# Two residual blocks with MLA and RWKV7 mixers: the FFN's first products by Strassen's scheme on pairs of tiles

## Chip, cores and metric

One Trainium2 chip, one of its cores (core 0). The metric is the device time of one execution in microseconds (us); lower is better. TensorE is the matmul engine, VectorE, ScalarE and GpSimd work on tiles, SyncE issues most transfers.

## Reference

Two blocks on x of 512 tokens by 1024 features, all in float32. Each block is an FFN, a mixer and a second FFN, each behind an RMS norm with a shift and a scale and with a gate that come from a vector c through `ada_w` (the modulation). The first block's mixer is latent attention (MLA), the second's RWKV7. An FFN is what the change is about:

```python
def _swiglu(h, w_in, w_out):
    gt, up = jnp.split(h @ w_in, 2, axis=-1)
    return (jax.nn.silu(gt) * up) @ w_out

x = x + 0.5 * mods[:, 0, 2][:, None, :] * _swiglu(h, w_in, w_out)
```

`h` has 1024 features, the inner width is 2816, so `w_in` is 1024 x 5632 and `w_out` 2816 x 1024. The program has four FFNs, one after the other with the mixers between: FFN, MLA, FFN, FFN, RWKV7, FFN.

## The kernel before, in words

Activations lie feature-major: a tile has 128 features on the partitions and 512 tokens along it. 1024 features are 8 tiles (`KT`), the inner width is 22 (`NF`). Float32 accuracy comes from splitting every operand into a high part and a rest (`float32r`) and adding three products: high by high, high by rest, rest by high (`mm3`, L268 to L274). So each product of a weight tile and an activation tile is three matmuls, and each matmul has its own weight load. A run of up to eight weight tiles of 128x128 (1024 columns) is loaded into a slot of `wraw` (three slots) by SyncE's queue (L245 to L249), ScalarE writes its high part `wh` (L262) and VectorE the rest `wl` (L266); `wh` and `wl` have three slots each.

An FFN (`ffn`, L477) goes in two halves of 11 inner tiles. For two inner tiles at a time it runs gate and up (u = 0, 1): 8 weight tiles of each, all 512 tokens, into four banks of PSUM (L502 to L504). ScalarE takes the silu of the gate (L507), VectorE multiplies it by up (L508), and `split` (L276) writes the high part (ScalarE, L279) and the rest (VectorE, L280) as `act`. After a half, `down` (L394) forms the eight output tiles from the 11 `act` tiles and adds each, times its gate, to x (`add_x`, L390 to L392). So x gets two additions for each of its tiles in an FFN. In the second half the last two output tiles go by halves of the tokens (256 columns, weights kept by `tail_weights`), so that the next norm's first half can start while the second half of them is multiplied; the last matmuls cover the norm (`_Norm.half`). The first products of the next FFN are by halves of the tokens too (L497 to L500). In the first FFN, the first four inner tiles come from `start` (L1481), which lays out norm, loads and products by hand.

The modulation vectors are 128 further tiles of 128x1024 (`mod_steps`, L359): each is loaded into a slot of `wraw` and reduced by one VectorE instruction with an accumulator (L366). `pump` (L381) issues them in small numbers between the pairs and the output tiles of the FFNs, until none is left.

Outside `start`, the last tiles before RWKV and RWKV itself, the order in which each engine takes its instructions is laid out by a scheduler when the program is built, from the order of the program and from the slots that are free; on the chip each engine keeps that order. Slots are shared by tag: `t` has 22 slots of two tiles (x, h, act and others), `s` 18 of one tile, `k` two of three tiles, and the PSUM tags `A` to `D` two banks each (L38). The numbers of a pair's products and the banks they go to:

```python
order = [(k, f, u, slice(0, S)) for f in fs for u in range(2) for k in range(KT)]
for k, f, u, sl in order if w else ():
    self.mm3(p[f, u], w[f, u][0][:, k], w[f, u][1][:, k], h[k], k == 0, k == KT - 1, sl)
```

## Time and profile before

| | |
|---|---|
| time, median of three runs | 2253.03 us (2250.35 to 2255.33) |
| span of the profiled execution, first to last instruction | 2255.1 us |
| TensorE busy | 96% |
| VectorE, ScalarE, GpSimd busy | 56%, 37%, 14% |
| mean granted clock of TensorE | 0.983 of 2.4 GHz |

The profile records the span of its execution, which lies inside the range of the runs; no other time is given for that execution. PE in the rows is TensorE's matmuls, PEld its weight loads, DVE VectorE, ACT ScalarE, POOL GpSimd, SP SyncE. A busy time counts an instruction from its start to its end, and instructions that are pipelined overlap: the start of one to the start of the next tells what it costs in a row. A matmul is busy for 0.39 us at 512 columns and 0.28 at 256, which is its latency. "x2" in a timeline merges two instructions of a kind. PEclk is the granted clock as a share of 2.4 GHz.

### The profile page before, as it was taken

The numbers are of one execution on the slowest core, as the hardware profiler recorded it, in microseconds if no ns is written. First come the engines' busy times: TensorE is split into PE (matmuls) and PEld (weight loads), VectorE is DVE, ScalarE is ACT, GpSimd is POOL, SyncE is SP. The second block draws the span as 40 slices with busy tenths as digits, with TensorE's granted clock in tenths as the row PEclk, the third lists the DMA queues.
The fourth block names the chain that finished last, engine by engine and source line by source line (L and its number), as shares of the span: only waits on it lengthen the run. The fifth ranks groups of instructions, "written<-read, shape, count | busy, mean of one in ns | idle before, by whom it ended". The sixth has DMA issues, their size and how long they took to land.

```text
span 2255.1 us, 29276 instructions
## 1 busy us (share of the span) xinstructions
PE 2165.5 (96%) x11089; PEld 1825.0 (81%) x11089; DVE 1252.3 (56%) x2247; ACT 841.7 (37%) x1403; POOL 324.9 (14%) x370
## 2 busy tenths in 40 slices
PE   6999999999999999999999998899789999999998
PEld 5778888878798888888888887677678879888887
DVE  8655555678665545556433337936946666333334
ACT  3322223467533222333222225756445444222222
POOL 5000001023200000010000003514575000000001
PEclk9999999999999999999999999999889999999999
DMA  8665666201325656645433332254686342323322
GB/s 283 196 196 171 203 202 192 81 32 34 129 85 191 200 180 203 189 131 168 126 99 103 95 108 88 75 168 142 181 245 165 96 146 85 95 86 110 96 84 82
DMA packets 150732, 312.25 MB, mean 138 GB/s; under 512 B 54784, under 2 KB 70432, under 8 KB 150592
## 3 DMA queue, kind: packets, MB, share of 16 engines
q1 hardware_dynamic: 149856, 309.68, 44.7%
q8 instruction: 87, 1.43, 0.3%
q10 hardware_dynamic: 576, 0.52, 0.1%
q14 instruction: 53, 0.43, 0.1%
q0 software_dynamic: 160, 0.19, 0.0%
HBM read 279.93 MB, written 30.41 MB: 138 GB/s over the span
## 4 chain that ended last, share of the span: by engine, by line
PE 82%; DVE 9%; DMA 3%; ACT 3%; issue 2%; POOL 1%; SPq 0%; DVEq 0%; ACTq 0%; POOLq 0%
PE up L272 13%; PE up L274 13%; PE up L273 13%; PE dn L272 8%; PE dn L273 8%; PE dn L274 8%; PE pr L168 4%; PE q L168 2%; PE a L168 2%; PE s L168 1%; PE o L168 1%; DVE ada L168 1%; DVE rsq_u L168 1%; PE ys L168 1%; DMA wraw<-in_ffn_in_dram 1%
## 5 line engine op out<-in xcount | busy, mean ns | idle before, releaser
L262 ACT ACTIVATE wh<-wraw 128x1024 fp32r<-128x1024 f32 (+2 forms) x307 | 292.8, 954 | 919.6 <-PE dn L273 274.4
L272 PE MATMUL up<-h,wh 128*128 128x512 f32 (+1 forms) x1416 | 536.3, 379 | 1.9 <-ACT silu L507 1.9
L273 PE MATMUL up<-h,wh 128*128 128x512 f32 (+1 forms) x1416 | 536.5, 379 | 0.0
L274 PE MATMUL up<-h,wl 128*128 128x512 f32 (+1 forms) x1416 | 535.9, 379 | 0.0
L266 DVE TENSOR_TENSOR wl<-wraw,wh 128x1024 fp32r<-128x1024 f32 (+2 forms) x307 | 334.6, 1090 | 325.4 <-ACT wh L262 322.5
L272 PEld LDWEIGHTS up<-h,wh 128*128 128x128 f32 x1416 | 266.7, 188 | 51.9 <-ACT silu L507 2.3
L273 PEld LDWEIGHTS up<-h,wh 128*128 128x128 f32 x1416 | 266.8, 188 | 49.7
L274 PEld LDWEIGHTS up<-h,wl 128*128 128x128 f32 x1416 | 266.4, 188 | 49.7
L366 DVE SCALAR_TENSOR_TENSOR wraw<-wraw,cact 128x1024 f32<-128x1024 f32 x128 | 158.0, 1235 | 180.5 <-DMA wraw<-in_ada_w_dram 179.4
L65 POOL TENSOR_TENSOR sq<-sq,sq 128x512 f32<-128x512 f32 x29 | 39.8, 1373 | 1494.3 <-ACT sq L61 1478.9
L272 PE MATMUL dn<-act,wh 128*128 128x512 f32 x627 | 244.7, 390 | 2.7 <-ACT act L279 2.7
L273 PE MATMUL dn<-act,wh 128*128 128x512 f32 x627 | 244.6, 390 | 0.3 <-DVE act L280 0.3
L274 PE MATMUL dn<-act,wl 128*128 128x512 f32 x627 | 244.7, 390 | 0.0
L272 PEld LDWEIGHTS dn<-act,wh 128*128 128x128 f32 x627 | 118.1, 188 | 27.8 <-ACT act L279 3.1
L273 PEld LDWEIGHTS dn<-act,wh 128*128 128x128 f32 x627 | 118.1, 188 | 25.2 <-DVE act L280 0.6
L274 PEld LDWEIGHTS dn<-act,wl 128*128 128x128 f32 x627 | 118.0, 188 | 24.5
L508 DVE TENSOR_TENSOR silu<-silu,up 128x512 f32<-128x512 f32 x88 | 60.2, 685 | 127.6 <-PE up L274 126.2
L392 DVE SCALAR_TENSOR_TENSOR x<-dn,mod,x 128x512 f32<-128x512 f32 (+1 forms) x91 | 61.6, 678 | 119.4 <-PE dn L274 119.1
L168 DVE TENSOR_TENSOR wl<-wraw,wh 128x1024 fp32r<-128x1024 f32 (+2 forms) x51 | 57.3, 1126 | 64.9 <-ACT wh L168 64.6
L168 PE MATMUL pr<-xs,wh 128*128 128x512 f32 (+1 forms) x242 | 78.0, 404 | 8.9 <-ACT xs L168 3.6
L279 ACT ACTIVATE act<-silu 128x512 fp32r<-128x512 f32 x88 | 55.2, 628 | 50.3 <-DVE silu L508 49.3
L168 PEld LDWEIGHTS pr<-xs,wh 128*128 128x128 f32 x242 | 47.0, 205 | 18.4 <-ACT xs L168 3.7
(414 smaller groups left out, 3494.9 us busy)
## 6 DMA issues: line engine op xcount, KB each, us to landing
wraw<-in_ffn_in_dram SPq DMA_DIRECT2D x168, 512.0 KB, 3.8
wraw<-in_ada_w_dram SPq DMA_DIRECT2D x128, 512.0 KB, 3.8
wraw<-in_ffn_out_dram SPq DMA_DIRECT2D x64, 384.0 KB, 3.1
wraw<-in_ffn_out_dram SPq DMA_DIRECT2D x64, 320.0 KB, 2.9
wraw<-in_rwkv_rkv_dram SPq DMA_DIRECT2D x24, 512.0 KB, 3.6
ada<-in_ada_w_dram SPq DMA_DIRECT2D x16, 512.0 KB, 6.0
bakd<-bak SPq DMA_DIRECT2D x32, 192.0 KB, 3.9
bak<-bakd SPq DMA_DIRECT2D x8, 768.0 KB, 6.3
```

What stands on the lines that cost most here:

```text
L65: nc.gpsimd.tensor_tensor(self.acc, self.acc, sq, op=ALU.add)
L168: self.tc.keep_in_program_order(op(*args, **kw))
L262: self.nc.scalar.activation(wh[:, :n], raw[:, :n], AF.Copy)
L266: self.nc.vector.tensor_tensor(wl[:, :n], raw[:, :n], wh[:, :n], op=ALU.subtract)
L272: mm(ps, wh, ah, start=first, stop=False)
L273: mm(ps, wh, al, start=False, stop=False)
L274: mm(ps, wl, ah, start=False, stop=last)
L279: nc.scalar.activation(hi[rows, sl], src, AF.Copy)
L366: nc.vector.scalar_tensor_tensor(raw2, raw2, 1.0, self.cact, op0=ALU.mult, op1=ALU.mult, accum_out=m[:, j - j0:j - j0 + 1])
L392: self.nc.vector.scalar_tensor_tensor(x, ps[:, sl], g[:, m:m + 1], x, op0=ALU.mult, op1=ALU.add)
L508: nc.vector.tensor_tensor(sl, sl, p[f, 1], op=ALU.mult)
```

## The change

Pairs of inner tiles are multiplied by Strassen's scheme (in Winograd's form). For gate and for up, the weights of a pair are a 2 x 2 matrix of quarters (two inner tiles by two halves of the 1024 features), and h is one of two halves of the features by two halves of the tokens. Seven products of quarters take the place of eight: each is 4 weight tiles by 256 tokens. The sums of weight quarters (s1 to s4) are formed by GpSimd and then split into high part and rest; the sums of activation quarters are formed once in an FFN by `activation_sums` (GpSimd rebuilds h from its parts, VectorE subtracts and splits). Products are accumulated in three banks X, Y and Z; between them ScalarE copies a bank to SBUF (c11, c12, p5, c22) and VectorE or GpSimd adds.

Pair 0 of each FFN stays as it was (`pair_plain`), and so do the pairs 0 and 1 of the first FFN, which come from `start`. The second product is done in five parts of two, two, two, two and three pairs (`PARTS`); the first four use `down_part`, which loads the weights of two output tiles at once, the last uses `down` as before with 6 inner tiles for 11. The raw weights of the second tile of a pair take a slot of the tag `k`. `wh` and `wl` get five slots for three; to make room, two small tiles of MLA move to the tag `s` and GpSimd's scratch for transfers shrinks, with the five setup loads moving from GpSimd's queue to ScalarE's. Cut to its core (comments that were removed are left out):

```diff
+PARTS = (0, 1), (2, 3), (4, 5), (6, 7), (8, 9, 10)
...
-        wh = self.wp.tile([P, 8, P], F32R, name=f"wh_{self.n}", tag="wh", bufs=3)
-        wl = self.wp.tile([P, 8, P], F32R, name=f"wl_{self.n}", tag="wl", bufs=3)
+        wh = self.wp.tile([P, 8, P], F32R, name=f"wh_{self.n}", tag="wh", bufs=5)
+        wl = self.wp.tile([P, 8, P], F32R, name=f"wl_{self.n}", tag="wl", bufs=5)
...
     def ffn(self, l, j, norm, nxt):
-        nc = self.nc
         s = 2 * j
-        h = norm.h
-        for half in range(2):
+        done = NS // 2 if norm.first else 1
+        for part in PARTS:
             act = []
-            f_end = (half + 1) * NH
-            f0 = half * NH
-            while f0 < f_end:
-                fs = range(f0, min(f0 + 2, f_end))
-                w, p = {}, {}
-                if f0 == 0 and norm.first:
-                    fs, p = range(NS), norm.first
+            for g in part:
+                if g == 0:
+                    self.pair_plain(l, j, norm, act)
+                elif g < done:
+                    self.pair_out(norm.first, 2 * g, act)
                 else:
-                    for f in fs:
-                        for u in range(2):
-                            first = f0 == 0 and norm.w
-                            w[f, u] = norm.w.pop(0) if first else self.wchunk(self.a["ffn_in"][l, j, f, u], KT)
-                            p[f, u] = self.ps("up", ("AB", "CD")[(f0 - half * NH) // 2 % 2][u])
-                if f0 == 0:
-                    order = [(k, f, u, HALF[0]) for k in range(KT) for f, u in THREE]
-                    order += [(k, f, u, HALF[1]) for k in range(KS) for f, u in THREE]
-                    order += [(k, f, u, HALF[1]) for f, u in THREE for k in range(KS, KT)]
-                    order += [(k, 1, 1, slice(0, S)) for k in range(KT)]
-                else:
-                    order = [(k, f, u, slice(0, S)) for f in fs for u in range(2) for k in range(KT)]
-                for k, f, u, sl in order if w else ():
-                    self.mm3(p[f, u], w[f, u][0][:, k], w[f, u][1][:, k], h[k], k == 0, k == KT - 1, sl)
-                for f in fs:
-                    sl = self.t("silu")
-                    nc.scalar.activation(sl, p[f, 0], AF.Silu)
-                    nc.vector.tensor_tensor(sl, sl, p[f, 1], op=ALU.mult)
-                    act.append(self.split(sl, "act", "u" if len(act) < 4 else "t"))
-                f0 += len(fs)
-                self.pump(4 if f0 > 2 else 0)
-
-            def chunks(m, half=half):
+                    self.pair_seven(l, j, g, norm, act)
+                self.pump(4 if g else 0)
+            k0, n = 2 * part[0] * P, 2 * len(part)
+            def chunks(m, k0=k0, n=n):
                 w = self.a["ffn_out"][l, j, m]
-                k0 = half * NH * P
-                return [(w[:, k0:k0 + 6 * P], 6), (w[:, k0 + 6 * P:k0 + NH * P], NH - 6)]
-
-            if half == 0:
-                self.down(chunks, act, (l, s))
+                if part is PARTS[-1] and (l, j) == (1, 0):
+                    return [(w[:, k0 + i * P:k0 + (i + n // 2) * P], n // 2) for i in (0, n // 2)]
+                return [(w[:, k0:k0 + n * P], n)]
+            if part is not PARTS[-1]:
+                self.down_part(self.a["ffn_out"][l, j], part[0] * 2, act, (l, s))
             else:
                 tail = (7,) if (l, j) == (1, 0) else (6, 7)
                 nx = nxt(tail)
                 self.down(chunks, act, (l, s), nx, tail)
         return nx
 
+    def down_part(self, w, f0, act, key):
+        self.mods_until(self.gate, key)
+        g, n = self.gate[key], len(act)
+        for m in range(0, KT, 2):
+            self.n += 1
+            raw = self.wp.tile([P, 8, P], F32, name=f"wraw_{self.n}", tag="wraw", bufs=3)
+            self.nc.sync.dma_start(raw.rearrange("p (m k) f -> p m (k f)", m=2),
+                                   w[m:m + 2, :, f0 * P:(f0 + n) * P].rearrange("m p f -> p m f"))
+            wh, wl = self.wsplit(raw, 2 * n)
+            for i in range(2):
+                ps = self.ps("dn", "ABC"[(m + i) % 3])
+                for k in range(n):
+                    self.mm3(ps, wh[:, i * n + k], wl[:, i * n + k], act[k], k == 0, k == n - 1)
+                self.add_x(m + i, ps, g)
+            self.pump(1)
+    def pair_out(self, p, f0, act):
+        nc = self.nc
+        for f in (f0, f0 + 1):
+            sl = self.t("silu")
+            nc.scalar.activation(sl, p[f, 0], AF.Silu)
+            nc.vector.tensor_tensor(sl, sl, p[f, 1], op=ALU.mult)
+            act.append(self.split(sl, "act", "u" if len(act) < 4 else "t"))
+    def pair_plain(self, l, j, norm, act):
+        h, p = norm.h, norm.first
+        if not p:
+            w, p = {}, {}
+            for f in range(2):
+                for u in range(2):
+                    w[f, u] = norm.w.pop(0) if norm.w else self.wchunk(self.a["ffn_in"][l, j, f, u], KT)
+                    p[f, u] = self.ps("up", ("AB", "CD")[f][u])
+            self.activation_sums(norm)
+            order = [(k, f, u, HALF[0]) for k in range(KT) for f, u in THREE]
+            order += [(k, f, u, HALF[1]) for k in range(KS) for f, u in THREE]
+            order += [(k, f, u, HALF[1]) for f, u in THREE for k in range(KS, KT)]
+            order += [(k, 1, 1, slice(0, S)) for k in range(KT)]
+            for k, f, u, sl in order:
+                self.mm3(p[f, u], w[f, u][0][:, k], w[f, u][1][:, k], h[k], k == 0, k == KT - 1, sl)
+        else:
+            self.activation_sums(norm)
+        self.pair_out(p, 0, act)
+    def activation_sums(self, norm):
+        nc, h = self.nc, norm.h
+        norm.sums7 = []
+        for i in range(KT // 2):
+            b = []
+            for k in (i, i + KT // 2):
+                b.append(self.t("hs"))
+                nc.gpsimd.tensor_tensor(b[-1], h[k][0].bitcast(F32), h[k][1].bitcast(F32), op=ALU.add)
+            norm.sums7.append(self.quarter_sums([x[:, sl] for x in b for sl in HALF]))
+    def quarter_sums(self, b):
+        nc = self.nc
+        b11, b12, b21, b22 = b
+        t = [self.t("ts").rearrange("p (a s) -> p a s", a=2) for _ in range(2)]
+        t1, t2, t3, t4 = (t[i // 2][:, i % 2] for i in range(4))
+        for out, x, y in ((t1, b12, b11), (t2, b22, t1), (t3, b22, b12), (t4, b21, t2)):
+            nc.vector.tensor_tensor(out, x, y, op=ALU.subtract)
+        hi, lo = (self.t2(n, F32R, "t").rearrange("p a (b s) -> p (a b) s", b=2) for n in ("tsh", "tsl"))
+        for i in range(2):
+            r = slice(2 * i, 2 * i + 2)
+            nc.scalar.activation(hi[:, r], t[i], AF.Copy)
+            nc.vector.tensor_tensor(lo[:, r], t[i], hi[:, r], op=ALU.subtract)
+        return [(hi[:, i], lo[:, i]) for i in range(4)]
+    def pair_seven(self, l, j, g, norm, act):
+        nc, free = self.nc, self.nc
+        K2 = KT // 2
+        q0, q1 = slice(0, K2), slice(K2, KT)
+        W = []
+        for u in range(2):
+            src = [self.a["ffn_in"][l, j, 2 * g + i, u].rearrange("p (k f) -> p k f", f=P) for i in range(2)]
+            ra = self.wraw(src[0], KT)
+            self.n += 1
+            rb = self.gp.tile([P, KT, P], F32, name=f"wrawb_{self.n}", tag="k", bufs=TAGS["k"])
+            nc.sync.dma_start(rb, src[1])
+            W.append((ra, rb))
+        w = [{} for _ in range(2)]
+        def keep(u, hl, *names):
+            for i, name in enumerate(names):
+                w[u][name] = tuple(x[:, i * K2:(i + 1) * K2] for x in hl)
+        sub = lambda out, x, y: nc.gpsimd.tensor_tensor(out, x, y, op=ALU.subtract)
+        S = []
+        for u, (ra, rb) in enumerate(W):
+            keep(u, self.wsplit(ra, KT), "a11", "a12")
+            st = self.t2("ws", F32, "t").rearrange("p a (k f) -> p (a k) f", f=P)
+            s2, s1 = st[:, q0], st[:, q1]
+            nc.gpsimd.tensor_tensor(s1, rb[:, q0], rb[:, q1], op=ALU.add)
+            sub(s2, s1, ra[:, q0])
+            sub(rb[:, q0], ra[:, q0], rb[:, q0])
+            S.append((st, s2))
+        for u in range(2):
+            keep(u, self.wsplit(S[u][0], KT), "s2", "s1")
+        for u in range(2):
+            keep(u, self.wsplit(W[u][1], KT), "s3", "a22")
+        for u in range(2):
+            a12 = W[u][0][:, q1]
+            sub(a12, a12, S[u][1])
+            hi, lo = (self.t(n, F32R).rearrange("p (k f) -> p k f", f=P) for n in ("s4h", "s4l"))
+            nc.scalar.activation(hi, a12, AF.Copy)
+            nc.vector.tensor_tensor(lo, a12, hi, op=ALU.subtract)
+            w[u]["s4"] = hi, lo
+        h, ts = norm.h, norm.sums7
+        X, Y, Z = (self.ps("up", tag) for tag in "ABC")
+        def product(ps, name, act_of, first=False):
+            for u in range(2):
+                for k in range(K2):
+                    wh, wl = (x[:, k] for x in w[u][name])
+                    ah, al = act_of(k)
+                    for n, (x, y) in enumerate(((wh, ah), (wh, al), (wl, ah))):
+                        ins = nc.tensor.matmul(ps[:, HALF[u]], x, y, start=first and u == k == n == 0,
+                                               stop=False, skip_group_check=True)
+                        self.tc.keep_in_program_order(ins)
+        quarter = lambda r, c: lambda k: tuple(x[:, HALF[c]] for x in h[k + r * K2])
+        tsum = lambda i: lambda k: ts[k][i]
+        copy = lambda name, ps: self._copy(name, ps)
+        product(X, "a11", quarter(0, 0), True)
+        c11 = copy("c11", X)
+        product(Y, "a12", quarter(1, 0), True)
+        nc.vector.tensor_tensor(c11, c11, Y, op=ALU.add)
+        product(X, "s2", tsum(1))
+        c12 = copy("c12", X)
+        product(Z, "s1", tsum(0), True)
+        p5 = copy("p5", Z)
+        product(X, "s3", tsum(2))
+        c22 = copy("c22", X)
+        nc.gpsimd.tensor_tensor(c22, c22, p5, op=ALU.add)
+        product(Z, "s4", quarter(1, 1))
+        nc.vector.tensor_tensor(c12, c12, Z, op=ALU.add)
+        product(X, "a22", tsum(3))
+        for top, bottom in (((c11, c12), None), ((X, c22), None)):
+            sl = self.t("silu")
+            for c, x in enumerate(top):
+                o = sl[:, HALF[c]]
+                nc.scalar.activation(o, x[:, HALF[0]], AF.Silu)
+                nc.vector.tensor_tensor(o, o, x[:, HALF[1]], op=ALU.mult)
+            act.append(self.split(sl, "act", "u" if len(act) < 4 else "t"))
+    def _copy(self, name, ps):
+        t = self.t(name)
+        self.nc.scalar.activation(t, ps, AF.Copy)
+        return t
...
-        sel = self.small("mla_sel", [P, P], bufs=1)
+        sel = self.t("mla_sel")[:, :P]
...
-        maskf = self.small("mla_maskf", [P, P], bufs=1)
+        maskf = self.t("mla_maskf")[:, :P]
...
-        nc.gpsimd.dma_start(self.ident, a["ident"])
+        nc.scalar.dma_start(self.ident, a["ident"])
...
-    nc = _bacc.Bacc("TRN2", target_bir_lowering=False, num_devices=1)
+    nc = _bacc.Bacc("TRN2", target_bir_lowering=False, num_devices=1, dynamic_dma_scratch_size=1024)
```

## Rows read from the trace of the kernel before

**Rows 1.** The page, part 1: busy us, share of the span, instructions.

```profile
PE 2165.5 (96%) x11089; PEld 1825.0 (81%) x11089; DVE 1252.3 (56%) x2247; ACT 841.7 (37%) x1403; POOL 324.9 (14%) x370
```

**Rows 2.** The four FFNs by windows: stretch, length, busy us, granted clock, transfers.

```profile
72.00:392.00 320.00, 313.88 (x1396) 259.70 (x1397) 177.78 (x251) 92.12 (x125) 7.21 (x6) 0.99 0.62 193
626.00:996.00 370.00, 369.07 (x1784) 311.65 (x1782) 208.28 (x328) 108.64 (x153) 10.24 (x10) 1.00 0.56 174
1004.00:1370.00 366.00, 365.68 (x1732) 307.55 (x1730) 149.83 (x224) 105.47 (x143) 9.18 (x7) 1.00 0.37 114
1880.00:2240.00 360.00, 359.88 (x1711) 302.93 (x1711) 130.67 (x190) 102.14 (x141) 7.97 (x7) 1.00 0.29 88
```

**Rows 3.** Who waited for whom, TensorE: us in total, times, longest.

```profile
PE dn L272 <- ACT act L279: 2.7, 1, 2.7
```

**Rows 4.** Timeline, TensorE: start us, length us, instruction, wait before it.

```profile
73.40 0.50 PE L272 MATMUL up<-h,wh 128*128 128x512 f32 x1 [1.86 <-ACT silu L507]
```

**Rows 5.** Timeline, TensorE at 512 columns: first and last of eight.

```profile
151.32 0.39 PE L272 MATMUL dn<-act,wh 128*128 128x512 f32 x1
...
152.91 0.39 PE L273 MATMUL dn<-act,wh 128*128 128x512 f32 x1
```

**Rows 6.** Timeline, TensorE at 256 columns: first and last, eighteen steps apart.

```profile
1005.80 0.28 PE L272 MATMUL up<-h,wh 128*128 128x256 f32 x1
...
1007.96 0.28 PE L272 MATMUL up<-h,wh 128*128 128x256 f32 x1
```

**Rows 7.** Timeline, VectorE: low part of weights, two gate products.

```profile
72.89 1.22 DVE L266 TENSOR_TENSOR wl<-wraw,wh 128x1024 fp32r<-128x1024 f32 x1 [0.43 <-ACT wh L262]
74.04 1.28 DVE L508 TENSOR_TENSOR silu<-silu,up 128x512 f32<-128x512 f32 x2
```

**Rows 8.** Timeline, GpSimd and VectorE side by side, two stretches.

```profile
48.84 2.00 POOL L1529 TENSOR_TENSOR hn<-hn,rb 128x512 f32<-128x512 f32 x1
...
49.62 2.31 DVE L168 SCALAR_TENSOR_TENSOR ada<-ada,cact 128x1024 f32<-128x1024 f32 x1
...
1536.03 1.29 POOL L168 TENSOR_TENSOR ag<-a,Gi 128x512 f32<-128x512 f32 x1 [15.91 <-ACT Gi L168]
1537.28 1.26 POOL L168 TENSOR_TENSOR AR<-r,G 128x512 f32<-128x512 f32 x1
1539.32 1.28 POOL L168 TENSOR_TENSOR kf<-r,km 128x512 f32<-128x512 f32 x1 [0.78 <-DVE km L168]
...
1539.98 0.69 DVE L168 TENSOR_TENSOR kk<-kk,rn 128x512 f32<-128x512 f32 x1 [0.73 <-PE rn L168]
```

**Rows 9.** Timeline, VectorE: an addition to x.

```profile
358.68 0.75 DVE L392 SCALAR_TENSOR_TENSOR x<-dn,mod,x 128x512 f32<-128x512 f32 x1 [1.04 <-PE dn L274]
```

**Rows 10.** Timeline, VectorE: low parts of the norm's two halves.

```profile
1002.87 1.27 DVE L106 SCALAR_TENSOR_TENSOR h<-hn,mod,h 128x256 fp32r<-128x256 f32 x3
...
1017.38 1.27 DVE L106 SCALAR_TENSOR_TENSOR h<-hn,mod,h 128x256 fp32r<-128x256 f32 x3
```

**Rows 11.** L366 alone by windows: stretch, length, VectorE's busy us, instructions, clock, transfers.

```profile
72.00:392.00 320.00, 66.79 (x108) 0.99 0.62 193
...
630.00:996.00 366.00, 72.57 (x116) 1.00 0.56 175
```

**Rows 12.** Timeline, TensorE: last product of the tail's first half.

```profile
997.00 0.28 PE L274 MATMUL dn<-act,tw 128*128 128x256 f32 x1
```

**Rows 13.** Window around the wait of rows 4, columns as in rows 2.

```profile
72.00:76.00 4.00, 2.60 (x7) 2.10 (x8) 3.47 (x5) 3.08 (x6) 0.00 (x0) 0.75 0.74 245
```

**Rows 14.** Groups of instructions by shape, ScalarE: busy us, mean ns, idle before.

```profile
L262 ACT ACTIVATE wh<-wraw 128x1024 fp32r<-128x1024 f32 x187 | 198.2, 1061 | 578.8 <-PE up L273 210.1 <-issue 160.3 <-DMA wraw<-in_ffn_in_dram 143.9
L279 ACT ACTIVATE act<-silu 128x512 fp32r<-128x512 f32 x88 | 55.2, 628 | 50.3 <-DVE silu L508 49.3
...
L168 ACT ACTIVATE A<-a 128x512 f32<-128x512 f32 x32 | 18.9, 592 | 1.7 <-PE a L168 1.5
```

**Rows 15.** Timeline, ScalarE: its first square of x.

```profile
4.57 1.15 ACT L1508 ACTIVATE sq<-x 128x512 f32<-128x512 f32 x2 [2.32 <-DMA x<-in_x_dram]
```

8 lines of the change are left out of this document (4 added, 4 removed).

## The prediction

> **What bounds the kernel now.** I read the page's engine totals first: TensorE is busy for 96% of the span [rows 1]. Then the four FFN stretches by window: in each of them TensorE is busy for 98% or more, at the full clock of 2.4 GHz, while VectorE is busy for 36 to 56% and GpSimd does almost nothing [rows 2]. The waits of TensorE in the FFNs come to two of note, 2.7 us [rows 3] and 1.86 us [rows 4]. So an FFN costs what its matmuls cost. The timeline of TensorE gives their price, start to start: eight starts of 512 columns from 151.32 to 152.91, so 1.59 / 7 = 0.227 us each [rows 5]; eighteen steps of 256 columns from 1005.80 to 1007.96, so 0.120 us each, each with a weight load of its own [rows 6].
>
> The second thing to see is how VectorE and GpSimd stand to each other. On GpSimd a 128x512 sum takes 1.25 us start to start (1536.03 to 1537.28) [rows 8]. In the start of the kernel a VectorE product of 128x1024, 1.22 us elsewhere [rows 7], took 2.31 from 49.62: it waited for the GpSimd sum of 48.84, which ended at 50.84 and had itself taken 2.00. But a product with one operand in PSUM (rn) took its 0.69 us in the middle of a GpSimd sum [rows 8]. So operations with two operands in SBUF and GpSimd's sums take turns; those that read PSUM pass.
>
> **TensorE's part of the change.** A pair of inner tiles had 2x2x8x3 = 96 matmuls of 512 columns, 21.8 us; it gets 7x2x4x3 = 168 of 256, 20.2 us. That is 1.6 us less for each of 9 + 10 + 10 + 10 = 39 pairs (pairs 0 and 1 of the first FFN and pair 0 of the others stay plain): **-63 us**. The second product keeps its matmuls. The Trainium skill, page "TensorE: Matmul & The Clock Gate", sections "LDWEIGHTS (loading the stationary operand)" and, in Part 3, "The mechanism", says that a load of 128 columns takes 128 / 1.2 = 107 ns and overlaps a matmul only in another row group; by that, 72 more loads cost 72 x 0.107 = 7.7 us a pair, an estimate from the page, and the sum of this part would be (7.7 - 1.6) x 39 = +238 us. The trace doesn't agree: 0.120 us with a load in each.
>
> **VectorE's part.** Starts of 128x1024 low parts lie 1.15 us apart, of 128x512 0.60 (two in 1.28 busy) [rows 7]; an addition to x is 0.75 busy, 0.68 in a row [rows 9]; 256 columns cost 0.40 (three in 1.27) [rows 10]. A pair of seven needs six low parts of 1024 (6.9), two of 512 for s4 (1.2), two additions of PSUM to c11 and c12 (1.2), four gate products of 256 (1.6), two low parts of act (1.2): 12.1 us, where it was 7.0. A part of two pairs needs four low parts for the down weights and eight additions to x: 10.0 us, and eight additions for each of five parts are 40 for 16 before. The modulation tiles, 1024 wide and so also 1.15, are pumped in the first two FFNs almost alone: 54 and 58 of the 128 now (each counts twice in the view, with its accumulator read) [rows 11]. After, 4 for a pair and 4 for a part: about 62 in each, 12 for a part of two pairs (13.8 us).
>
> **GpSimd's part.** Four sums of 512 for each of gate and up, and c22: nine a pair, 18 x 1.25 = 22.5 us a part, all from SBUF, so all taking turns with VectorE.
>
> A part in the first two FFNs then asks of TensorE 2 x 20.2 + 21.8 = 62.1 us (65.4 before), of VectorE 24.2 + 10.0 + 13.8 = 48.0 and of GpSimd 22.5. In turns that is 70.5. What can pass (c11, c12, half of the gate products, the additions to x) is 2.4 + 1.6 + 5.4 = 9.4, so 61.1 if all of it passes. **The two engines together become the bound there.** In the last two FFNs, without modulation, 56.7 stays under 62.1.
>
> For the whole first FFN (72 to 392 us, 320): VectorE nine pairs 109, the plain pairs 5, sums of the activations 4 x (4 x 0.40 + 2 x 0.60) = 11, down 40 + 12.5, modulation 71: 248; GpSimd 95 sums, 119; together 367, less 47 that can pass 320. TensorE would need 320 - 9 x 1.6 = 306. I take halfway, 344, since GpSimd has work waiting most of the time but VectorE's passing operations need not fall beside it: **+24**. The second FFN (370): VectorE 266, GpSimd 130, together 396, passing 51, so 345; TensorE 354. Between 354 and 396 I take 375: **+5**. The third and fourth (366 and 360): -16 each, **-32**.
>
> **Waits that the change adds.** Ahead of the third product of the first pair of seven, the sums of the activations must be there; they can begin when the fifth low part of the norm's second half is there, the second of the three from 1017.38 [rows 10], 12 us after the FFN's first matmul at 1005.80 [rows 6], and take 4 x (2 x 1.25 + 2.8) = 21 us in turns, while the plain pair and two products cover 21.8 + 5.8 from that matmul. With the other work on VectorE I put 6 us (0 to 12) each on FFNs three and four: **+12** (the second has it in its bound, the first has a down product to cover it).
>
> At an FFN's end the half tail that covers the next norm shrinks from 2 x 11 x 3 x 0.120 = 7.9 us to 4.3. The norm's first half took from the last product of its half at 997.0 until the first low part at about 1003.3 [rows 10, 12], 6.3 us, so 2 us show three times: **+6** (0 to 12, as a wait can cost clock too: the wait of 1.86 us lies in a stretch with a mean granted clock of 0.75 [rows 13], that is partly at 1.2 GHz).
>
> At a part's end the second product has nine matmuls, 2.0 us, before it needs the last act tile, whose chain (gate product, high, low part) is 0.40 + 0.63 + 0.60 and handing over: 0.5 us for 5 parts in two FFNs, **+5** (0 to 15). ScalarE rises by two wh, two highs of s4 and four copies a pair, 2 x 1.06 + 2 x 0.63 + 4 x 0.59 = 5.7 us [rows 14]; it has room for that by its busy time [rows 2], but the copies read PSUM between products into the same bank; each has a product in another bank to cover it, 24 x 0.120 = 2.9 us, but stands on ScalarE behind wh of tiles that wait for GpSimd. I put 0.2 us (0 to 1.0) on 20 pairs: **+4**.
>
> At nothing: SP's queue carries the same weights; rb waits there for one of two slots, with later loads behind it, covered while the weights are a pair ahead, and 3.8 us for each load behind it if not. Five setup loads go from GpSimd's queue to ScalarE's, ahead of its first square, which waits 2.32 us for x now [rows 15] and covers most of five issues. The wh and wl slots (5 for 3), the DMA scratch and MLA's small tiles stand on no wait of the rows. I put -3 to +3 on all of these.
>
> **The sum.** 24 + 5 - 32 + 12 + 6 + 5 + 4 = +24 on the profiled execution, whose span is 2255.1: 2279. The median of the three runs, 2253.03, lies 2.1 lower, so **2277 us**.
>
> **Rivals.** A, the forecast: turns bind the first two FFNs halfway; 2245 to 2315. Chance 0.50. B, faster: GpSimd's sums slip into what passes and into VectorE's idle time. Then the first FFN is at 320 (0), the second at TensorE's 354 (-16), the others at -16 + 3 each, and the norm's end adds 6: 0 - 16 - 26 + 6 = -36, 2217. It decides where more than some 35 of the 47 us that can pass in the first FFN do. For it: VectorE is idle for 44% of the first FFN now [rows 2]; against it: that idle time is what the new work fills. Chance 0.33. C, in turns entirely, and ScalarE's copies of PSUM late by 1 us in the 20 pairs of the last FFNs, because the wh in front of them waits for GpSimd: 47 + 26 - 32 + 12 + 6 + 5 + 20 = +84, 2337. For it: five engines in order, each with a short queue of slots. Chance 0.16. D: the change doesn't save on TensorE, because 256 columns don't hide a weight load. A load is busy for 259.70 / 1397 = 0.186 us [rows 2]; 72 of them in the open are 13.4 us a pair, less 1.6, times 39: +460, 2713. The 0.120 us of rows 6 speak against it. Chance 0.01. The Trainium skill's page "TensorE: Matmul & The Clock Gate" has this rule.
>
> **How the numbers follow.** What a measurement can tell is about 0.2%, 4.5 us. Of A 0.44 is slower, 0.05 within, 0.01 faster; B is faster; C and D slower: 0.34, 0.05, 0.61. The range reaches from just under B, where waits at the handovers are nil, to just under C: 2212 to 2332, leaving a part of C, D and the best of B outside. A's own range is 2245 to 2315.
>
> **What would show it.** Right: matmuls of 256 at 0.120 us; VectorE at 75% or more in the first two FFNs, with GpSimd's 128x512 sums well over 1.29 us and VectorE's 1024 operations often at 2.3; the first FFN longer than 320 us, the last two shorter than 366 and 360, and TensorE's granted clock below full in the first two. Wrong: GpSimd's sums at 1.3 us and TensorE at 98% in the first FFN (B), or waits of TensorE on ScalarE's copies in the last two FFNs (C).

## The result, and the profile after

The changed kernel takes **2499.86 us** (median of four runs, 2488.96 to 2503.81) against 2253.72 before: a ratio of 1.1087, 95% interval 1.106 to 1.1113. "Slower" was right; the size was not, since 2500 lies far above the range's end of 2332. The profiled execution took 2488.96, its span is 2487.2, 232.1 longer than before.

The page's totals, in the columns of [rows 1]:

```profile
PE 2181.4 (88%) x13792; PEld 1954.0 (79%) x13792; DVE 1750.9 (70%) x2721; ACT 1070.4 (43%) x1795; POOL 956.5 (38%) x748
```

TensorE is busy for about as long as before (2165.5) in a span that is 10% longer: it waits. Where, the four FFNs by windows tell, in the columns of [rows 2], each from the FFN's first matmul (the first FFN from 72 us) to the next stage's first:

```profile
72.00:482.40 410.40, 329.14 (x2092) 301.54 (x2091) 317.49 (x404) 148.62 (x219) 154.78 (x90) 0.90 0.51 170
724.40:1164.50 440.10, 374.27 (x2440) 343.64 (x2438) 342.96 (x446) 164.28 (x246) 178.52 (x106) 0.93 0.46 151
1164.50:1572.90 408.40, 366.32 (x2425) 338.22 (x2425) 260.84 (x337) 167.33 (x257) 166.33 (x109) 0.95 0.26 86
2073.60:2487.20 413.60, 363.84 (x2450) 335.01 (x2448) 256.18 (x339) 160.28 (x240) 161.15 (x106) 0.96 0.24 78
```

Cut at the same places, the FFNs took 329.2, 366.3, 369.1 and 375.6 before: **+81, +74, +39 and +38**. MLA has +4 and RWKV -4. So the last two, which were to gain 16 each, lose as well. VectorE is busy for 77% and 78% of the first two, as forecast, and the granted clock is down to 0.90 to 0.96, where it was 0.99 to 1.00. Who waited for whom, TensorE (us in total, times, longest), in place of the one line of [rows 3]:

```profile
PE up L631 <- ACT c L662: 88.5, 21, 7.0
PE up L631 <- DVE wl L268: 36.1, 3, 13.3
PE dn L274 <- ACT wh L264: 35.9, 4, 30.9
PE dn L275 <- DVE act L282: 21.5, 22, 2.3
```

Three waits stand out. The largest is for ScalarE's copy of a product out of PSUM (L662), an instruction of 0.6 us that I had given 0.2 us of lateness. The second comes three times, once at the start of each FFN but the first, inside the *first* product of the first pair of seven: after the gate's twelve matmuls and two of up's, TensorE waits for the low part of up's weights. The third, 30.9 us, comes once, in the first FFN.

**The low part at an FFN's start.** VectorE and then TensorE in the third FFN (start, length, instruction, wait before it):

```profile
1180.50 0.73 DVE L573 TENSOR_TENSOR ts<-hs 128x256 f32<-128x256 f32 x1
...
1205.17 1.28 DVE L578 TENSOR_TENSOR tsl<-ts,tsh 128x512 fp32r<-128x512 f32 x2
...
1207.58 1.21 DVE L268 TENSOR_TENSOR wl<-wraw,wh 128x1024 fp32r<-128x1024 f32 x1
```

```profile
1208.85 0.58 PE L631 MATMUL up<-h,wl 128*128 128x256 f32 x1 [13.33 <-DVE wl L268]
```

VectorE worked without a pause of note from 1180.50. The activations' sums (`ts` and their low parts `tsl`) took it until 1206.45, and the low part that TensorE wanted since 1195.52 stood behind them. So TensorE didn't wait for the sums as operands, but for a weight's low part in VectorE's order.

**The copy, followed back.** One such wait in the third FFN, TensorE's timeline (start, length, instruction, wait before it), with what the clock does after it:

```profile
1422.42 0.39 PE L631 MATMUL up<-tsh,wh 128*128 128x256 f32 x1 [2.42 <-ACT c L662]
...
1422.87 0.28 PE L631 MATMUL up<-tsh,wh 128*128 128x256 f32 x1
1422.99 0.28 PE L631 MATMUL up<-tsl,wh 128*128 128x256 f32 x1
...
1423.96 0.41 PE L631 MATMUL up<-tsh,wh 128*128 128x256 f32 x1
1424.17 0.42 PE L631 MATMUL up<-tsl,wh 128*128 128x256 f32 x1
```

ScalarE in the same stretch:

```profile
1408.51 0.60 ACT L662 ACTIVATE c<-up 128x512 f32<-128x512 f32 x1 [1.41 <-PE up L631]
...
1415.01 0.42 ACT L656 ACTIVATE silu<-c 128x256 f32<-128x256 f32 x1 [5.60 <-POOL c L648]
...
1421.25 0.63 ACT L281 ACTIVATE act<-silu 128x512 fp32r<-128x512 f32 x1 [0.59 <-DVE silu L657]
1421.78 0.58 ACT L662 ACTIVATE c<-up 128x512 f32<-128x512 f32 x1
```

And GpSimd, which makes c22:

```profile
1399.92 1.91 POOL L606 TENSOR_TENSOR ws<-wrawb 128x512 f32<-128x512 f32 x1 [18.57 <-DMA wrawb<-in_ffn_in_dram]
...
1407.52 2.27 POOL L606 TENSOR_TENSOR ws<-wrawb 128x512 f32<-128x512 f32 x1
...
1412.44 1.29 POOL L600 TENSOR_TENSOR wraw<-wraw,ws 128x512 f32<-128x512 f32 x1
1413.70 1.28 POOL L648 TENSOR_TENSOR c<-c,p 128x512 f32<-128x512 f32 x1
```

From the end backwards: the copy that TensorE wants at 1420 starts at 1421.78, as ScalarE works through what stood ahead of it since 1415.01. There the gate's silu of the pair before (L656) had waited 5.60 us for c22. c22's operand was copied by 1409.11, but the addition (L648) comes on GpSimd behind the eight weight sums of the *next* pair, which run from 1399.92 to 1413.70. These began so late because GpSimd had waited 18.57 us for the second raw tile, rb. And rb had been issued only at 1396.29; SP's queue let go of three such loads in the 25 us from there, since each waits for a slot:

```profile
1396.29 24.99 SPq L592 DMA_DIRECT2D wrawb<-in_ffn_in_dram  x3
```

This is no single case. By the waits of ScalarE, GpSimd and SP's queue, the silu waited for c22 37 times, the first sum for rb 39 times, and rb's load (L592) 74 times for the low part that frees its slot. ScalarE also waited 31 times for the last sum of a weight, whose high part (s4h) it takes before later copies:

```profile
ACT silu L656 <- POOL c L648: 170.6, 37, 10.6
...
ACT s4h L618 <- POOL wraw L600: 90.9, 31, 7.2
...
POOL ws L606 <- DMA wrawb<-in_ffn_in_dram: 405.1, 39, 21.1
...
SPq L592 <- DVE wl L268: 578.4, 74, 58.9
```

Some waits cost more than their length. Behind the 2.42 us the matmuls of 256 columns go on at 0.120 us for a while, and from 1423.96 to 1427.36 at 0.21: the lower level, 1.2 GHz. Not every wait does this: after one of 2.43 us, which ended at 2261.96 in the fourth FFN, the granted clock stayed at 1.00. The six us behind either wait, in the columns of [rows 2]:

```profile
1422.40:1428.40 6.00, 5.98 (x37) 5.99 (x38) 4.22 (x5) 2.46 (x3) 1.27 (x1) 0.72 0.90 289
...
2261.90:2267.90 6.00, 5.94 (x49) 5.95 (x50) 4.23 (x5) 3.25 (x5) 1.29 (x1) 1.00 0.87 297
```

Of the last two FFNs' ten waits for these copies, each of 2.1 to 2.8 us, five were followed by the lower level.

**The sums' own length.** The groups on GpSimd and VectorE show the turns: four kinds of sums of 128x512, 1.25 us in [rows 8], and low parts of 128x1024, 1.22 in [rows 7] (busy us, mean ns):

```profile
L600 POOL TENSOR_TENSOR ws<-ws,wraw 128x512 f32<-128x512 f32 x78 | 138.0, 1769 | 92.9 <-DMA wraw<-in_ffn_in_dram 89.8
...
L268 DVE TENSOR_TENSOR wl<-ws,wh 128x1024 fp32r<-128x1024 f32 x78 | 115.2, 1478 | 15.6 <-ACT wh L264 15.6
```

### The profile page after: what moved, and what is told of

It is laid out like the page before. It is cut to its first block, busy times and chain, and to the rows that moved or that the text cites. A ratio compares the mean times of both kernels' runs of the same rounds, so it can differ in the third digit from the quotient of the medians.

```text
span 2487.2 us, 36102 instructions
## 1 busy us (share of the span) xinstructions
PE 2181.4 (88%) x13792; PEld 1954.0 (79%) x13792; DVE 1750.9 (70%) x2721; ACT 1070.4 (43%) x1795; POOL 956.5 (38%) x748
## 3 DMA queue, kind: packets, MB, share of 16 engines
q8 instruction: 108, 1.77, 0.3%
## 4 chain that ended last, share of the span: by engine, by line
PE 31%; DVE 11%; POOL 7%; ACT 4%; issue 3%; DMA 2%; SPq 0%; POOLq 0%; ACTq 0%; DVEq 0%
PE up L631 8%; PE pr L170 4%; PE dn L275 4%; PE dn L276 3%; PE dn L274 3%; DVE wl L268 2%; PE a L170 2%; POOL wraw L600 2%; POOL ws L600 1%; POOL ws L606 1%; DVE ts L573 1%; ACT wh L264 1%; PE q L170 1%; POOL wrawb L600 1%; DVE act L282 1%
## 5 line engine op out<-in xcount | busy, mean ns | idle before, releaser
L631 PE MATMUL up<-tsh,wh 128*128 128x256 f32 x1248 | 371.6, 298 | 88.5 <-ACT c L662 88.5
L631 PE MATMUL up<-tsl,wh 128*128 128x256 f32 x1248 | 368.2, 295 | 0.0
L631 PE MATMUL up<-tsh,wl 128*128 128x256 f32 x1248 | 367.6, 295 | 0.0
L606 POOL TENSOR_TENSOR ws<-wrawb 128x512 f32<-128x512 f32 x78 | 136.5, 1752 | 533.4 <-DMA wrawb<-in_ffn_in_dram 405.1
L631 PEld LDWEIGHTS up<-tsh,wh 128*128 128x128 f32 x1248 | 255.5, 205 | 93.0 <-ACT c L662 92.8
L631 PEld LDWEIGHTS up<-tsl,wh 128*128 128x128 f32 x1248 | 255.3, 205 | 0.2
L631 PEld LDWEIGHTS up<-tsh,wl 128*128 128x128 f32 x1248 | 254.8, 204 | 0.0
L631 PE MATMUL up<-h,wh 128*128 128x256 f32 x1248 | 230.2, 286 | 0.0
L368 DVE SCALAR_TENSOR_TENSOR wraw<-wraw,cact 128x1024 f32<-128x1024 f32 x128 | 178.0, 1392 | 57.2 <-DMA wraw<-in_ada_w_dram 56.9
L631 PE MATMUL up<-h,wl 128*128 128x256 f32 x624 | 179.3, 287 | 36.1 <-DVE wl L268 36.1
L631 PEld LDWEIGHTS up<-h,wh 128*128 128x128 f32 x1248 | 199.6, 196 | 1.5
L600 POOL TENSOR_TENSOR ws<-ws,wraw 128x512 f32<-128x512 f32 x78 | 138.0, 1769 | 92.9 <-DMA wraw<-in_ffn_in_dram 89.8
```

The lines of the kernel that those rows point to most:

```text
L368: nc.vector.scalar_tensor_tensor(raw2, raw2, 1.0, self.cact, op0=ALU.mult, op1=ALU.mult, accum_out=m[:, j - j0:j - j0 + 1])
L600: sub = lambda out, x, y: nc.gpsimd.tensor_tensor(out, x, y, op=ALU.subtract)
L606: nc.gpsimd.tensor_tensor(s1, rb[:, q0], rb[:, q1], op=ALU.add)
L631: ins = nc.tensor.matmul(ps[:, HALF[u]], x, y, start=first and u == k == n == 0, stop=False, skip_group_check=True)
```

## The experiments

Two theories stood at the outset. *Turns*: GpSimd's sums and VectorE's operations with two operands in SBUF block each other, as my sum had it, only more. *Order*: engines work their instructions in a fixed order, and one that waits for a late sum holds all behind it (the expectations also call it the blocked queue; "theory 1" of the later runs is the sums and the chain of work behind them). All are single runs beside one of the kernel before on the same chip (2250.41, 2256.49 and 2252.81 us in the three lots), so some 6 us between runs of different lots say nothing. The first table builds the change up, the second undoes its parts; lengths of the four FFNs in us, cut as above. For the change the time is the median of its runs, 2499.86; its FFNs are those of the profiled execution, 2488.96, so a gain that I give against the median is up to 11 us less against that execution.

| built up | time | FFN 1 | 2 | 3 | 4 |
|---|---|---|---|---|---|
| before | 2253.72 | 329.2 | 366.3 | 369.1 | 375.6 |
| five parts alone | 2286.68 | 344.0 | 370.8 | 371.9 | 380.6 |
| and the seven products, no sums | 2247.24 | 339.5 | 366.2 | 356.0 | 365.7 |
| and the activations' sums | 2312.06 | 361.8 | 382.5 | 370.1 | 377.0 |
| and short weight sums | 2317.41 | 363.7 | 383.5 | 372.8 | 379.8 |
| the change | 2499.86 | 410.4 | 440.1 | 408.3 | 413.6 |

| undone in the change | time | FFN 1 | 2 | 3 | 4 |
|---|---|---|---|---|---|
| c22 on VectorE | 2453.65 | 406.0 | 438.5 | 390.9 | 397.8 |
| four slots for high and low parts | 2507.13 | 407.5 | 434.5 | 421.5 | 429.8 |
| four, and three k slots | 2441.22 | 391.8 | 417.2 | 405.6 | 410.4 |
| four, three k slots, c22 on VectorE | 2397.13 | 384.4 | 409.4 | 392.4 | 397.2 |
| all sums and c22 on VectorE | 2359.86 | 369.7 | 392.9 | 383.9 | 392.1 |
| no activation sums | 2424.89 | 392.5 | 421.0 | 391.1 | 403.2 |
| short modulation | 2461.67 | 391.8 | 422.4 | 410.8 | 416.5 |
| idle sums | 2547.40 | 417.4 | 448.5 | 426.1 | 434.8 |

**Five parts alone.** Plain pairs, no sums.

```diff
-        K2 = KT // 2
...
+                w[f, u] = self.wchunk(self.a["ffn_in"][l, j, f, u], KT)
...
+        self.pair_out(p, 2 * g, act)
```

> The second product in five parts stays, the pairs are plain again: no sums of weights or of activations. Theory 1 (the loss comes with the sums and the chain that waits for them): the third and fourth FFN come back to 369 to 377 us each (369.1 and 375.6 before), since five handovers instead of two cost about 1 us each, and the time is about 2260 to 2285. Rival (the five parts cost by themselves, each handover some 5 us of TensorE): every FFN is 15 us or more longer than before, 2310 or more. For the first FFN, which loses 30.9 us before its first down product: if the activations' sums cause that, it comes to 330 to 340 us; if the eight modulation tiles do, which stand ahead of the down weights, it stays at about 360.

2286.68, 30 more than the kernel before beside it: 2 us over theory 1's range, and far under the rival's. FFNs two to four lose 3 to 5 us each, the first 15, and 8.4 of these are one wait of TensorE for the first down weights; with 344.0 it lies between the two guesses for it, near the one that blames the activations' sums. So the five parts are no bargain, but an eighth of the loss.

**The products without any sums.** No weight sums (the next diff) and no activations' sums; a quarter of the pair's weights and of h stands where a sum would.

```diff
-            self.activation_sums(norm)
...
-        tsum = lambda i: lambda k: ts[k][i]
+        tsum = lambda i: quarter(i // 2, i % 2)
```

> No sums at all, neither of weights nor of activations (the products take the unsummed quarters): the seven products, their copies and additions and the five parts stay. If TensorE's 1.6 us a pair is really saved and the copies of PSUM cost nothing, 2286.68 (five parts alone) - 63 = 2224, within 12. If the copies and the hand-over of the banks X, Y and Z give it back, 2270 or more.

2247.24, halfway between the two: 39 of the 63 us come back. The last two FFNs give what was worked out, 15.9 and 14.9 for 16; the first two give 4.5 and 4.6. There, and not in the last two, TensorE still waits for ScalarE's copies, 7.5 us in eight waits, and for the second product's act tiles, 16.4 us. The windows of the last two FFNs beside the change's above: TensorE at 98% and 96% with a clock of 0.99 and 0.98.

```profile
1021.10:1377.10 356.00, 350.34 (x2424) 327.39 (x2424) 215.57 (x313) 163.93 (x249) 23.50 (x21) 0.99 0.31 98
1879.70:2245.40 365.70, 352.53 (x2450) 329.46 (x2448) 214.06 (x315) 157.26 (x232) 21.62 (x18) 0.98 0.27 88
```

In the third FFN the change is 52.4 us longer than this run: by the two rows TensorE is idle for 36.4 us more, and its matmuls are busy for 16.0 us more, at a clock of 0.95 for 0.99.

This run is also the ceiling of what this arrangement can bring: with every sum for nothing it is 5.6 us, 0.25%, under the kernel before, hardly more than single runs can tell.

**No weight sums**, with the activations' sums made.

```diff
-            st = self.t2("ws", F32, "t").rearrange("p a (k f) -> p (a k) f", f=P)
-            s2, s1 = st[:, q0], st[:, q1]
-            nc.gpsimd.tensor_tensor(s1, rb[:, q0], rb[:, q1], op=ALU.add)
-            sub(s2, s1, ra[:, q0])
-            sub(rb[:, q0], ra[:, q0], rb[:, q0])
-            S.append((st, s2))
+            S.append((ra, ra[:, q0]))
...
-            sub(a12, a12, S[u][1])
```

> The eight sums of weight quarters of a pair are left out (the products take unsummed quarters, so the output is another); c22 and the activations' sums stay on GpSimd, and VectorE, ScalarE and TensorE have the same work as in the changed kernel. Both the theory of turns and that of the blocked queue: the loss goes away nearly whole, total 2210 to 2280. If it stays above 2400, the loss comes from the longer work of VectorE and ScalarE and from slots, not from GpSimd's sums.

2312.06, 32 over the 2280 that both theories gave at most: they had left the activations' sums out. Against the change the eight weight sums of a pair are worth 188 us; against the run without any sums, those of the activations, of which there are only 4 x 4 sets in the whole kernel, are worth 65: 22, 16, 14 and 11 by FFN. (The tile ws goes with the sums here, and frees slots.)

**Short sums.** All weight sums in their places, of 64 columns each.

```diff
-            nc.gpsimd.tensor_tensor(s1, rb[:, q0], rb[:, q1], op=ALU.add)
-            sub(s2, s1, ra[:, q0])
-            sub(rb[:, q0], ra[:, q0], rb[:, q0])
-            S.append((st, s2))
+            nc.gpsimd.tensor_tensor(s1[:, :, :16], rb[:, q0, :16], rb[:, q1, :16], op=ALU.add)
+            sub(s2[:, :, :16], s1[:, :, :16], ra[:, q0, :16])
+            sub(rb[:, q0, :16], ra[:, q0, :16], rb[:, q0, :16])
+            S.append((rb, s2[:, :, :16]))
...
-            sub(a12, a12, S[u][1])
+            sub(a12[:, :, :16], a12[:, :, :16], S[u][1])
```

> The eight weight sums of a pair stay on GpSimd, in the same order and with the same waits and slots, but each adds 64 columns in place of 512 (the products take the unsummed tile ra and a tile rb of which only these columns are summed, so the output is another one). Theory 1 (the length of the sums, in turns with VectorE and in the chain behind them): close to the run without sums, 2312 to 2360. Rival (order, handing over and slots by themselves, whatever a sum's length): 2420 or more.

2317.41, 5 above the run without them, as theory 1 had it. So the order, the waits and the slots cost next to nothing by themselves; they cost once the sums are long. The four kinds of sums took 0.50 to 0.68 us here and 1.66 to 1.77 in the change. GpSimd's wait for rb is even longer than in the change, and does no harm, as so little work comes behind it:

```profile
L606 POOL TENSOR_TENSOR ws<-wrawb 128x64 f32<-128x64 f32 x78 | 49.7, 639 | 591.4 <-DMA wrawb<-in_ffn_in_dram 591.4
```

**No activations' sums**, all weight sums. The diff is that of the products without sums.

> The sums of the activations are left out (the products take the unsummed quarters of h), all weight sums stay. Theory 1: the starts of the four FFNs, which wait 30.9 us in the first and about 13 us in the others, come back, and some of the turns there: 50 to 80 us less than the changed kernel, 2420 to 2450, with about 10 us left of the first FFN's wait, for which the modulation tiles ahead of the down weights stand (8.4 us in the run of the five parts alone). Rival: the weight sums, late by themselves, take the place of that wait, and less than 25 us comes back.

2424.89, 75 less, and the first FFN keeps a wait of 8.9 us for the down weights where the change has 30.9:

```profile
PE up L628 <- ACT c L659: 85.7, 20, 7.8
...
PE dn L274 <- ACT wh L264: 8.9, 1, 8.9
```

These are theory 1's numbers. The copies stay late by themselves (85.7 for 88.5 us); the waits for the first pair's low parts are all but gone (1.6 us).

**c22 on VectorE.**

```diff
-        nc.gpsimd.tensor_tensor(c22, c22, p5, op=ALU.add)
+        nc.vector.tensor_tensor(c22, c22, p5, op=ALU.add)
```

> Only the addition c22 += p5 moves from GpSimd to VectorE. The theory of the blocked queue (on GpSimd c22 stands behind the next pair's eight sums, ScalarE's silu waits for it and holds the next pair's copy of X, for which TensorE waits): the third and fourth FFN, 408 and 414 us, fall to 375 or less, the total to 2350 to 2420. The theory of turns (VectorE and GpSimd share their reads of SBUF and are the bound by their sum): one sum in nine moves, 39 x 1.25 us less on GpSimd and 39 x 0.6 more on VectorE, so the total falls by no more than 30 us, to 2460 or more.

2453.65, 46 under the median (35 under the profiled execution), though VectorE has an operation more and GpSimd runs the same eight sums a pair. That lies between the two theories: more than the turns gave, and far less than the order did, whose 375 us for each of the last two FFNs are missed by 16 and 23. TensorE's wait for the copies falls to 55.3 us. The gain is in the last two FFNs (17 and 16); what sets the time in the first two (4 and 2) was not tried by itself. ScalarE's other wait for GpSimd, for the sum behind s4h, is left as it was, 88.6 us.

**Four slots for high and low parts**, the comparison for the next run.

```diff
-        wh = self.wp.tile([P, 8, P], F32R, name=f"wh_{self.n}", tag="wh", bufs=5)
+        wh = self.wp.tile([P, 8, P], F32R, name=f"wh_{self.n}", tag="wh", bufs=4)
...
```

> Four slots for high and low parts in place of five, nothing else: the comparison for the run with three k slots. I expect 2490 to 2520, 0 to 30 us longer than the changed kernel, since a pair holds three tiles each of gate and up and fewer of the next pair's can be made ahead.

2507.13, 7 above the median. MLA is back at 238.8 us (238.2 before, 242.0 in the change), so its 4 us go with the fifth slot.

**Three k slots**, with four for the high and low parts.

```diff
-TAGS = {"t": 22, "u": 4, "s": 18, "k": 2, "A": 2, "B": 2, "C": 2, "D": 2}
+TAGS = {"t": 22, "u": 4, "s": 18, "k": 3, "A": 2, "B": 2, "C": 2, "D": 2}
...
```

> Three slots for the second raw weight tile of a pair in place of two, and four of five slots for the high and low parts to make room. Theory 1a (the sums start late because their second tile is loaded late, as it waits for a slot): faster than the run with four slots alone by 40 us or more, about 2450. Theory 1b (GpSimd's and ScalarE's order holds everything, the load is late only as a result): within 15 us of the run with four slots alone.

2441.22, 66 less than with four slots alone: the late load is a cause. GpSimd's wait for it, with two slots and with three:

```profile
POOL ws L606 <- DMA wrawb<-in_ffn_in_dram: 501.4, 41, 18.6
```

```profile
POOL ws L606 <- DMA wrawb<-in_ffn_in_dram: 257.3, 32, 10.7
```

**Both**, the three k slots (with four for the high and low parts) and c22.

```diff
-TAGS = {"t": 22, "u": 4, "s": 18, "k": 2, "A": 2, "B": 2, "C": 2, "D": 2}
+TAGS = {"t": 22, "u": 4, "s": 18, "k": 3, "A": 2, "B": 2, "C": 2, "D": 2}
...
-        nc.gpsimd.tensor_tensor(c22, c22, p5, op=ALU.add)
+        nc.vector.tensor_tensor(c22, c22, p5, op=ALU.add)
```

> Both repairs of the order at once: c22's addition on VectorE and three slots for the second raw tile (four for high and low parts). Alone they were worth 46 us (2453.65 against 2499.86) and 66 us (2441.22 against 2507.13). If they are two separate waits, 2507 - 66 - 46 = about 2395, within 15; if they are two views of one chain (late sums hold c22), 2430 or more. What is then left above the 2359.86 of the run with all sums on VectorE is the price of the turns between GpSimd and VectorE: 35 us by the first, 70 or more by the second.

2397.13 where two separate waits gave 2395. The lateness of rb and c22's place behind the sums are two costs, 110 us together. Only the totals add up so well: c22's part is 7 to 8 us in each of the first two FFNs here, 4 and 2 without the third slot.

**All sums and c22 on VectorE**, the activations' sums too.

```diff
-        sub = lambda out, x, y: nc.gpsimd.tensor_tensor(out, x, y, op=ALU.subtract)
+        sub = lambda out, x, y: nc.vector.tensor_tensor(out, x, y, op=ALU.subtract)
...
```

> All sums of the pairs (weights, activations, c22) move from GpSimd to VectorE. The theory of turns: a sum costs VectorE 0.6 us in place of 1.25 of GpSimd's turn, a part in the first two FFNs asks 48 + 11 = 59 us of VectorE against 62 of TensorE, so the FFNs come to TensorE's time with some waits: total 2220 to 2290. The theory of the blocked queue: the same gain as in e1 and a little more, since the long queue is gone from GpSimd but stands on VectorE: 2300 to 2400. A third theory, that VectorE in its fixed order is the bound whatever GpSimd does: 2450 or more.

2359.86, in the range of the blocked queue and not in that of the turns: the best of the runs that make every sum, and still 4.9% above the kernel before beside it. A VectorE that is busier (1771.0 us for 1750.9) but takes no turns with weight sums does better than the two engines together: its low parts of 128x1024 from wraw are back at a mean of 1.23 us (1.48 in the change). That the 37 us to the run with both repairs are what GpSimd's slower sums and the turns still cost is likely, but not shown: the two runs also differ in their slots.

**Idle sums.** GpSimd makes as many sums of a constant tile, which nobody reads, and the products take unsummed quarters.

```diff
-            nc.gpsimd.tensor_tensor(s1, rb[:, q0], rb[:, q1], op=ALU.add)
...
+            c8 = self.cact.rearrange("p (k f) -> p k f", f=P)
+            sub(st[:, q1], c8[:, q0], c8[:, q1])
...
```

> GpSimd makes as many sums of the same size for each pair, but of a constant tile, into a tile that nobody reads; the products take the unsummed quarters, so neither ScalarE nor VectorE waits for a weight sum. c22 still stands behind these sums on GpSimd. Theory 1 (engines in a queue: what waits for a sum holds back what stands behind it): the two of them together, the weights' wait and c22's, are what is lost; without the first, near the run without sums, 2312 to 2380. Rival (turns: a sum stops VectorE's operations with two operands in SBUF, whoever reads it): the sums still take their turns, so the time stays at 2430 or more, and VectorE's low parts of 128x1024 stay at 1.3 us or more.

2547.40: slower than the change itself, on the side of the turns. Nothing holds these sums back, so they bunch at an FFN's start, behind the eight sums that rebuild h. Here GpSimd and then VectorE at the start of the third FFN (start, length, operation):

```profile
1196.63 9.94 POOL L563 TENSOR_TENSOR hs<-h 128x512 f32<-128x512 f32 x7 [2.39 <-DVE h L108]
1206.52 74.80 POOL L600 TENSOR_TENSOR ws<-cact 128x512 f32<-128x512 f32 x48
```

```profile
1203.91 1.50 DVE L573 TENSOR_TENSOR ts<-hs,ts 128x256 f32<-128x256 f32 x1
1205.33 1.52 DVE L573 TENSOR_TENSOR ts<-hs 128x256 f32<-128x256 f32 x1
1206.78 1.51 DVE L573 TENSOR_TENSOR ts<-hs,hs 128x256 f32<-128x256 f32 x1
...
1241.26 4.51 DVE L268 TENSOR_TENSOR wl<-wraw,wh 128x1024 fp32r<-128x1024 f32 x2
1245.69 4.53 DVE L268 TENSOR_TENSOR wl<-wrawb,wh 128x1024 fp32r<-128x1024 f32 x2
```

Operations of 256 columns start 1.42 us apart and low parts of 1024 2.2, with one GpSimd sum to each. TensorE waits 27.1 us there for one low part. Once that stretch is over, two pairs take their nominal 40.2 us (336 x 0.120): what counts is where the sums fall. As a test of the chain alone the run fails, since it moved the sums; and it doesn't show the turns alone either, since c22 now stands behind 48 sums, and TensorE's waits for the copies are 63.1 us in all, up to 21.3.

**Short modulation.** The modulation's product on 64 of its 1024 columns.

```diff
-            nc.vector.scalar_tensor_tensor(raw2, raw2, 1.0, self.cact, op0=ALU.mult, op1=ALU.mult,
+            nc.vector.scalar_tensor_tensor(raw2[:, :64], raw2[:, :64], 1.0, self.cact[:, :64], op0=ALU.mult, op1=ALU.mult,
...
```

> The modulation's products on VectorE are done for 64 of 1024 columns (the output is another), their loads stay. The theory of turns: 62 x 1.1 us of VectorE's turn go from each of the first two FFNs, which fall by 50 to 70 us each (from 410 and 440), the last two keep 408 and 414; total 2350 to 2390. The theory of the blocked queue: the first two fall only so far as the modulation delays GpSimd, by 10 to 30 us each; total 2430 to 2470.

2461.67, as the blocked queue had it. The first two FFNs are 19 and 18 us shorter, of the 155 that they lose, and the last two, where next to none of this work lies, 3 longer each. So VectorE's load has a part in the loss of the first two, and it is not the main one.

## Why the prediction failed, step by step

- **TensorE, -63: right as a price.** A matmul of 256 columns took 0.120 us and two pairs without late inputs 40.2, as worked out; the run without sums has 31 of the last two FFNs' 32 us. Rival D is out.
- **The first two FFNs' bound from turns, +24 and +5: the turns are there, the term is far too small.** They got +81 and +74: the five parts 15 and 4.5, the products -4.5 and -4.6, the activations' sums 22 and 16, the weight sums 49 and 58. The sum counted the work of VectorE and GpSimd in a stretch and let it fill the stretch evenly. With both repairs of the order, the second FFN still takes 409, which is over the 396 of turns in full: a total of work is a floor, and the lateness of one sum comes on top.
- **"In the last two FFNs, without modulation, 56.7 stays under 62.1", -32: the step that failed outright.** They got +77 in place of -32, by the runs: five parts 8, products -31, activations' sums 25, weight sums 75. An engine pair with spare time on average was still late each pair, as its work could start only when rb had landed.
- **At nothing: rb's wait for one of two slots, "covered while the weights are a pair ahead": wrong.** With the sums between the load and the product the weights were no pair ahead: the wait for rb is 405.1 us on GpSimd, and the third slot is worth 66 us of the kernel's time.
- **Not in the sum at all: c22's place on GpSimd**, behind the next pair's eight sums, and ScalarE's silu behind c22; worth 46 us. I had costed c22 as one more sum and not asked who waits for it.
- **ScalarE's copies, +4 on 20 pairs.** In the last two FFNs the waits for them come to 11.8 and 12.5 us, near rival C's 20; in the first two, where the sum had none, to 34.1 and 30.2. C named the right instruction and only part of the cause: it had the weights' high parts in front wait for GpSimd, as s4h did, 90.9 us in all, but the silu that waits for c22 is the longer, 170.6.
- **The activations' sums, +12 for the third and fourth: near in size, wrong in the path.** I had the third product wait for the sums. The waits, 13.3 and 11.2 us, are in the first product, for a weight's low part that stands behind the sums on VectorE; a kernel that makes this low part ahead of the sums was not run. The sums took VectorE 26 us in the third FFN (1180.50 to 1206.45) for my 21 "in turns", which counted one exchange for each of GpSimd's sums, while each of VectorE's operations beside them pays a turn, as the idle sums show. The second FFN, whose bound was to hold this wait, has 11.6.
- **"The first has a down product to cover it": wrong** by the 30.9 us of the first FFN's wait, 22 of which go with these sums; 8 to 9 stay in every run without them. The trace has the path. VectorE takes its first modulation product of this stretch (L368) at 84.00, behind the sums. Its tile holds a slot of `wraw`, for which SP's queue waited 19.7 us, the longest of its waits for such a product. Five modulation loads go out from 85.25, ahead of the down weights, which are issued at 96.99, and TensorE starts at 102.98. That the 8 to 9 us are the modulation tiles ahead of the down weights was not tried by itself; with their products short, 26.8 of the 30.9 us stay.

```profile
SPq L250 <- DVE wraw L368: 187.1, 94, 19.7
```

```profile
83.33 0.41 DVE L573 TENSOR_TENSOR ts<-hs,hs 128x256 f32<-128x256 f32 x1
83.67 0.41 DVE L573 TENSOR_TENSOR ts<-hs,ts 128x256 f32<-128x256 f32 x1
84.00 1.21 DVE L368 SCALAR_TENSOR_TENSOR wraw<-wraw,cact 128x1024 f32<-128x1024 f32 x1
...
85.25 10.92 SPq L250 DMA_DIRECT2D wraw<-in_ada_w_dram  x5
...
96.99 0.38 SPq L516 DMA_DIRECT2D wraw<-in_ffn_out_dram  x1
...
101.88 1.06 ACT L264 ACTIVATE wh<-wraw 128x1024 fp32r<-128x1024 f32 x1 [10.04 <-DMA wraw<-in_ffn_out_dram]
...
102.98 0.80 PE L274 MATMUL dn<-act,wh 128*128 128x512 f32 x1 [30.87 <-ACT wh L264]
```

- **Handovers and the norm's end, +11.** The five parts alone cost 12 us in FFNs two to four, and 6 in the first besides its wait for the down weights, 18 to 19 in all: short, but of the right order. The 4 us in MLA, which go with the fifth slot, I had at nothing.
- **The clock** was in the range as a remark and not in the sum. The granted 0.90 to 0.96 is a cost that many of these waits bring along: 16.0 of the third FFN's 52.4 us against the run without sums.

## What to carry to other kernels

A trade of matmuls for additions is paid for by the length of the additions and by the order in which they get done, which here was worth 110 us, and the share of busy time tells neither: follow each new operand from its load's slot to the instruction that reads it, on every queue, and ask what stands behind each one that waits. An accumulating step that the next stage needs soon doesn't belong behind prefetch work of the same engine. Before tuning such a scheme, run it with the additions left out: here the ceiling was 0.25%.

## What the runs showed of the hardware

A VectorE operation with two operands in SBUF, beside an unbroken row of GpSimd sums, pays about 1.1 us whatever its size: 1.42 us from start to start for 256 columns (0.34 for the same operation while GpSimd is idle, at 83.33 in the first FFN of the change) and 2.2 for 1024 (1.15 alone, [rows 7]). A sum on GpSimd starts every 1.56 us on average in that row (74.80 / 48; part of it runs beside nothing), against 1.25 alone. The Trainium skill, page "SBUF — State Buffer", section "Who interferes with whom", has this as an exclusive lock on ports that the two engines share, which the one that issues first holds for the whole instruction. The trace agrees with the taking of turns, though the exchange of 1.42 us is shorter than the two lengths together, 1.25 + 0.34 = 1.59.

A GpSimd sum of 64 columns took 0.50 to 0.68 us, where 512 take 1.25: an eighth of the columns in about half of the time. And a wait of 2.42 us was followed by 3.4 us at the lower clock level, which began 1.5 us after the matmuls had resumed, while another of 2.43 us was followed by none.
